# Half products of a 7-product matmul with moving operand and PSUM output taken from the last column to the first

## The chip, the cores and the metric

The kernel runs on one core of a Trainium2 chip. The metric is the device time of one execution in microseconds; the profile is that of one such execution, recorded by the hardware. A core has five engines with a queue of instructions each: TensorE (PE in the profile, its weight loads PEld), VectorE (DVE), ScalarE (ACT), GpSimd (POOL) and SyncE (SP), which issues DMAs. TensorE multiplies a stationary operand, held in its array, with a moving operand that it streams from SBUF column by column, and adds the result into PSUM.

## The reference, cut to what matters

One decoder layer on a sequence of 512 positions with a model width of 1024: a pooling mixer and a sparse attention in parallel, merged by gates, then a gated MLP with a short convolution. All inputs are fp32. The change lies in the first matmul of the MLP, `h @ w_up`:

```python
x = x + (gate_pool * y_pool + gate_nsa * y_nsa) @ w_out[l]
h = rms_norm(x, ffn_norm_g[l])
gate_pre, val = jnp.split(h @ w_up[l], 2, axis=-1)      # 1024 -> 2 x 2816
gate_c = causal_dwconv(gate_pre, conv_w[l], conv_b[l])  # 3 taps along the sequence
x = x + (jax.nn.silu(gate_c) * val) @ w_down[l]
```

## The kernel before, in words

**Layout.** Activations lie transposed: a feature block of 128 on the partitions, the 512 positions along the free dimension. A matmul has a 128x128 block of weights as its stationary operand and positions as its moving operand. Every fp32 number is split into a high and a low part, both of the type fp32r, and a product is the sum of three matmuls, high x high, high x low and low x high. ScalarE makes the high part by a rounding copy, and the low part comes from VectorE by a subtraction or from ScalarE and a DMA of GpSimd that adds.

**The MLP's first matmul.** The 2816 gate features and the 2816 value features are 22 blocks each; block `f` of both is worked on together. The first four blocks (`up_plain`) use 8 blocks of the model width times 3 matmuls of 512 columns, for gate and for value: 48 matmuls. Blocks 4 to 21 (`up_fast`) treat the same work as a 2x2 by 2x2 block product (gate and value x the two halves of the model width, by the two halves of the model width x the two halves of the positions) and do it with 7 products in place of 8, after a scheme of the Strassen kind. Each of the 7 is a call of `product` (L1133): 4 blocks of the inner width, and in each 3 matmuls of 256 columns, 12 matmuls in all. The sums of weight blocks that the scheme needs are made on VectorE, ScalarE and GpSimd for each `f`; those of the activations are made once, in `halves` (tiles `nh`, `nl` for the blocks as they are, `th`, `tl` and two reused tiles `ot`, `oraw` for the sums). `mov` returns for each product the moving half tile, 256 columns that lie next to each other in SBUF. The output of a product is the first 256 columns of a PSUM bank, `bank_[:, :H2]`; there are three banks per `f` (`bx`, `by`, `bq`), and two or three products add into each, with reads by ScalarE or VectorE in between.

**What sets the order.** The program is first recorded: each engine call becomes an operation of a plan (`Plan.note`, L382 is where all of them are issued in the end, so that all instructions of the profile carry that line). The plan simulates the engines with its own prices, several times, and emits the order that came out best. All matmuls of one block of one product are one unit. The price of a matmul depends on the number of columns of its moving operand, and the overlap of two accesses on the span of columns that they touch. Which semaphores an instruction waits for is derived when the operations are issued. A buffer of PSUM that is used again is waited for as a tile: the new user waits for all users of the old one.

**Beside the products.** Between the products of `up_fast` stand pieces of the MLP's second matmul (`dn_group`, 512 columns each, bank `sc`), and products 6 and 7 of a block `f` run inside the next block. After the last block come the rest of the second matmul and the stores.

Of the kernel before, what the change touches and what calls it, by code (L numbers as in the profile page):

```python
# [385 lines left out]
def hybrid_layer(ctx: ExitStack, tc: tile.TileContext, xT, pos, par, cst, poolw, w1, wa, wb, wf,  # L386
# [3 lines left out]
    PE, ACT, DVE, POOL, SP = pl.engines  # L390
# [16 lines left out]
    def keep(name, shape, dt=F32, bufs=1):  # L407
        return pl.tile(sb, shape, dt, name, "t_" + name, bufs)
# [250 lines left out]
    for t in range(NT):  # L659
        x, y = qp[t], kp[t]  # L660
# [156 lines left out]
    x = keep("kcx", (64, 1, DH))  # L817
# [247 lines left out]
    H2 = T // 2  # L1065
# [41 lines left out]
    def split_y(f, y):  # L1107
        yh[f], yl[f] = page("yh", dt=F32R), page("yl", dt=F32R)
        split(yh[f], yl[f], y)

    def up_plain(f):
# [18 lines left out]
        DVE.tensor_mul(y, y, t)  # L1130
        split_y(f, y)

    def product(bank_, a, b, k0):  # L1133
        ah, al = a
        bh, bl = b
        for k in range(4):
            c = slice(k * P, (k + 1) * P)
            with pl.unit():
                for j, (w, x) in enumerate(((ah, bh), (ah, bl), (al, bh))):
                    PE.matmul(bank_[:, :H2], w[:, c], x(k), start=k0 and k == 0 and j == 0,  # L1140
                              stop=k == 3 and j == 2, skip_group_check=True)

    def mov(i, half):
# [34 lines left out]
    def up_fast(f, n1, n2, n3):  # L1178
# [30 lines left out]
        p1, u2, u3 = half[0][:, :H2], half[0][:, H2:], half[1][:, :H2]  # L1209
        g, y = page("fg"), page("y")  # L1210
        product(bx, halves_(a1, 0), mov(0, 0), True)
        begun.append(pl.last())
        ACT.activation(p1, bx[:, :H2], AF.Copy)
        more = list(held)
        del held[:]
        if more:
            more[0]()
        fill(n1, f == PLAIN)
        product(by, h2, mov(2, 1), True)
        DVE.tensor_add(u2, by[:, :H2], p1)  # L1220
        if more:
            more[1]()
        fill(n3)
        product(bq, h1, mov(2, 0), True)
        product(bx, halves_(a1, 1), mov(1, 0), False)
        ACT.activation(g[:, :H2], bx[:, :H2], AF.Copy)
# [133 lines left out]
```

## Time and profile before

| what | value |
|---|---|
| median of 3 runs | 706.78 us |
| lowest and highest | 706.33 and 707.64 us |
| profiled execution | 706.15 us, its span 704.4 us |
| mean granted clock of TensorE | 0.999 |
| TensorE busy | 697.2 us of the span, 4142 matmuls |
| VectorE, ScalarE, GpSimd busy | 492.7, 422.3 and 103.7 us |
| moved by DMA | 113.99 MB |

How to read it: a group of instructions is given with the engine, the operation, output and inputs by the names of their tiles (buffer numbers left out), the shapes, the count, then busy time in us and the mean duration of one in ns, and what the engine waited for before them. The duration of a matmul runs from its start until its last column is in PSUM; the next matmul starts earlier, so the distance between starts is shorter than the duration. A tile that is written in PSUM has the name of its bank's group (`mm`, `tr`, `av`, `sc`). The chain is followed back from the last instruction, at each step to what released it.

### The profile page before, as it was taken

Reading aid. Unit: us, or ns where it says so; the run is one execution under the profiler, and the core shown is the slowest. Engines: PE = TensorE matmul, PEld = TensorE weight load, DVE = VectorE, ACT = ScalarE, POOL = GpSimd, SP = SyncE. Lnnn points to the kernel's source line nnn. Section 1 sums busy time; section 2 is a strip of 40 time slices with the busy share of each in tenths; the row PEclk is TensorE's granted clock in tenths of the full one; section 3 lists DMA queues with packets and bytes.
Section 4 is the critical chain, followed back from the end, with each engine's and each line's share of the span. In section 5 each row is a group of like instructions: output and inputs, shape, how many; then the busy total and the mean of one; then the engine's idle time right before and its main releaser. Section 6 shows DMA issues by size and latency. Waiting matters only on the chain.

```text
span 704.4 us, 11308 instructions
## 1 busy us (share of the span) xinstructions
PE 697.2 (99%) x4142; PEld 615.6 (87%) x4142; DVE 492.7 (70%) x1060; ACT 422.3 (60%) x756; POOL 103.7 (15%) x127
## 2 busy tenths in 40 slices
PE   9999999999999999999999999999999999999997
PEld 8898888888888888888888899999989999999886
DVE  6768488887866653675569967886778777776632
ACT  8557367677776664333467857685757566673310
POOL 0001301010110000000021323231312112220000
PEclk9999999999999999999999999999999999999999
DMA  8477255454565567844369698989868666774131
GB/s 297 167 180 224 61 120 135 105 132 109 150 153 143 146 139 229 280 158 156 122 150 235 151 211 170 219 185 222 186 173 205 157 162 166 170 161 112 45 127 60
DMA packets 45272, 113.99 MB, mean 162 GB/s; under 512 B 5281, under 2 KB 5409, under 8 KB 45217
## 3 DMA queue, kind: packets, MB, share of 16 engines
q1 hardware_dynamic: 29232, 76.57, 33.6%
q0 software_dynamic: 15840, 36.71, 29.1%
q8 instruction: 32, 0.52, 0.3%
q14 instruction: 24, 0.19, 0.1%
q10 hardware_dynamic: 144, 0.01, 0.0%
HBM read 70.27 MB, written 6.29 MB: 109 GB/s over the span
## 4 chain that ended last, share of the span: by engine, by line
PE 88%; DMA 3%; issue 3%; DVE 3%; ACT 1%; POOL 1%; POOLq 0%; ACTq 0%; DVEq 0%
PE mm L382 39%; PE tr L382 28%; PE sc L382 12%; PE av L382 10%; DMA sl<-r 2%; DMA r<-wup 1%; DVE wlo L382 1%; DMA sl<-wraw 0%; ACT whi L382 0%; DVE y L382 0%; POOL tl L382 0%; POOL sl L382 0%; ACT ft L382 0%; ACT sh L382 0%; DVE kc L382 0%
## 5 line engine op out<-in xcount | busy, mean ns | idle before, releaser
L382 ACT ACTIVATE whi<-wraw 128x1024 fp32r<-128x1024 f32 (+1 forms) x96 | 97.9, 1019 | 74.4 <-issue 29.0
L382 DVE TENSOR_TENSOR wlo<-wraw,whi 128x1024 fp32r<-128x1024 f32 (+1 forms) x66 | 76.4, 1157 | 16.6 <-ACT whi L382 14.3
L382 POOL DMA_DIRECT2D wlo<-wraw x30 | 26.3, 875 | 332.0 <-ACT wlo L382 278.7
L382 PE MATMUL mm<-xh,whi 128*128 128x512 f32 x176 | 73.0, 415 | 0.3
L382 PE MATMUL mm<-xh,wlo 128*128 128x512 f32 x176 | 69.0, 392 | 0.0
L382 PE MATMUL mm<-xl,whi 128*128 128x512 f32 x176 | 69.0, 392 | 0.0
L382 PE MATMUL mm<-tl,sh 128*128 128x256 f32 x190 | 53.8, 283 | 0.0
L382 PE MATMUL mm<-th,sh 128*128 128x256 f32 x174 | 49.5, 285 | 1.3 <-DVE u L382 1.2
L382 PE MATMUL mm<-th,sl 128*128 128x256 f32 x174 | 49.3, 284 | 0.2 <-DMA sl<-r 0.2
L382 POOL DMA_DIRECT2D sl<-r x36 | 31.4, 872 | 72.8 <-ACT sl L382 46.7
L382 ACT ACTIVATE pp<-pp,asm 128x128 f32<-128x128 f32 (+3 forms) x64 | 35.4, 556 | 11.1 <-DVE asm L382 11.0
L382 DVE SCALAR_TENSOR_TENSOR ft<-fg,pr,ft 128x511 f32<-128x511 f32 (+1 forms) x44 | 33.0, 749 | 11.8 <-ACT ft L382 11.1
L382 PE MATMUL sc<-yh,whi 128*128 128x512 f32 x104 | 40.8, 392 | 0.0
L382 PE MATMUL sc<-yl,whi 128*128 128x512 f32 x104 | 40.8, 392 | 0.0
L382 ACT ACTIVATE wlo<-wraw 128x1024 fp32r<-128x1024 f32 x30 | 31.8, 1060 | 14.9 <-PE mm L382 6.0
L382 PE MATMUL sc<-yh,wlo 128*128 128x512 f32 x104 | 40.5, 389 | 0.0
L382 PEld LDWEIGHTS mm<-xh,wlo 128*128 128x128 f32 x176 | 33.0, 188 | 7.3
L382 PEld LDWEIGHTS mm<-xh,whi 128*128 128x128 f32 x176 | 33.2, 189 | 5.8 <-DVE th L382 1.0
L382 PEld LDWEIGHTS mm<-xl,whi 128*128 128x128 f32 x176 | 33.3, 189 | 4.0
L382 PEld LDWEIGHTS mm<-tl,sh 128*128 128x128 f32 x190 | 36.4, 192 | 0.4
L382 PEld LDWEIGHTS mm<-th,sh 128*128 128x128 f32 x174 | 33.2, 191 | 3.1 <-DVE u L382 1.9
L382 ACT ACTIVATE ft<-fg,pr 128x512 f32<-128x512 f32 x22 | 17.8, 811 | 27.6 <-DVE fg L382 22.0
(394 smaller groups left out, 2116.9 us busy)
## 6 DMA issues: line engine op xcount, KB each, us to landing
wlo<-wraw POOLq DMA_DIRECT2D x30, 512.0 KB, 4.5
wraw<-wup SPq DMA_DIRECT2D x26, 512.0 KB, 4.3
wraw<-wf SPq DMA_DIRECT2D x22, 512.0 KB, 3.4
r<-wup SPq DMA_DIRECT2D x36, 256.0 KB, 4.7
sl<-r POOLq DMA_DIRECT2D x36, 256.0 KB, 5.3
wraw<-wdn SPq DMA_DIRECT2D x16, 512.0 KB, 4.5
sl<-s POOLq DMA_DIRECT2D x18, 256.0 KB, 6.2
sl<-wraw POOLq DMA_DIRECT2D x18, 256.0 KB, 4.3
```

Source lines behind the costliest of these rows:

```text
L382: getattr(self.real[o.eng], method)(*a, **kw)
```

## The change

A new helper `back` takes a two-dimensional access pattern (partitions, then columns with step 1) and returns one over the same elements that starts at the last column and has the step -1. In `product`, the moving operand and the PSUM output of every matmul go through it. Column 255 of the moving half tile is read first and lands in column 255 of the output, column 0 comes last; each result stands where it stood. The stationary operand, every other matmul of the kernel and all readers of the banks keep their patterns.

```diff
+    def back(x):
+        n = x.ap[1][1]
+        return bass.AP(tensor=x.tensor, offset=x.offset + n - 1, ap=[list(x.ap[0]), [-1, n]])
+
     def product(bank_, a, b, k0):
         ah, al = a
         bh, bl = b
@@
             with pl.unit():
                 for j, (w, x) in enumerate(((ah, bh), (ah, bl), (al, bh))):
-                    PE.matmul(bank_[:, :H2], w[:, c], x(k), start=k0 and k == 0 and j == 0,
+                    PE.matmul(back(bank_[:, :H2]), w[:, c], back(x(k)), start=k0 and k == 0 and j == 0,
                               stop=k == 3 and j == 2, skip_group_check=True)
```

In the program that comes out, the instructions of every engine and their order are the same as before. TensorE's matmuls have 44 more waits on TensorE's own semaphore, and 6 more instructions that only wait for it.

## The prediction

> **What bounds the kernel now.** I read the page first, its busy shares, its slices and the chain that ended last.
>
> ```profile
> span 704.4 us, 11308 instructions
> ...
> PE 697.2 (99%) x4142; PEld 615.6 (87%) x4142; DVE 492.7 (70%) x1060; ACT 422.3 (60%) x756; POOL 103.7 (15%) x127
> ...
> PEclk9999999999999999999999999999999999999999
> ...
> DMA packets 45272, 113.99 MB, mean 162 GB/s; under 512 B 5281, under 2 KB 5409, under 8 KB 45217
> ...
> PE 88%; DMA 3%; issue 3%; DVE 3%; ACT 1%; POOL 1%; POOLq 0%; ACTq 0%; DVEq 0%
> ```
>
> TensorE is busy for 99% of the span, at full granted clock in every slice, and it is 88% of the chain. So the kernel is bound by the rate at which TensorE takes matmuls, and whatever each matmul costs more or less is paid almost in full. That must hold in the stretch that the change touches, so I asked for the groups by shape between 380 and 670 us, and for the busy time between 384 and 667 us.
>
> ```profile
> L382 PE MATMUL mm<-tl,sh 128*128 128x256 f32 x190 | 53.8, 283 | 0.0
> ...
> L382 PE MATMUL mm<-th,sh 128*128 128x256 f32 x174 | 49.5, 285 | 1.3 <-DVE u L382 1.2
> L382 PE MATMUL mm<-th,sl 128*128 128x256 f32 x174 | 49.3, 284 | 0.2 <-DMA sl<-r 0.2
> ...
> L382 PE MATMUL tr<-oraw,sl 128*128 128x256 f32 x2 | 0.6, 283 | 0.0
> ```
> ```profile
> 384.00:667.00 283.00, 281.50 (x1948) 1.00 0.74 170
> 667.00:704.40 37.40, 33.47 (x148) 0.98 0.26 88
> ```
>
> The view has 24 groups of shape 128x256 there; their counts add up to 1512 matmuls. That is what the code gives: features 4 to 21 are 18 features, each with 7 products of 4 blocks and 3 matmuls, 18 x 84 = 1512. The stretch is 283.00 us long and TensorE is busy for 281.50 of it, so 1.50 us of idle time is all that a slower matmul could hide in; the last 37.40 us have no half product in them.
>
> The mean of one (283 ns) is a latency: the next matmul starts long before. What counts is the distance between starts, and the chain in order of time gives it, for merged runs of matmuls. The first row below is a run of half products, the second one of 512 columns (the output projection).
>
> ```profile
> 411.73 5.76 PE tr L382 x48
> 307.16 5.44 PE mm L382 x24
> ```
>
> 5.76 / 48 = 120.0 ns for 256 columns; 5.44 / 24 = 226.7 ns for 512 columns. The difference is 106.7 ns for 256 columns, 0.417 ns per column, and what is left of the 120.0 ns is a fixed part of 13.3 ns. The half products cost 1512 x 120.0 ns = 181.4 us now.
>
> **The change, part by part.** (1) The helper that builds the two patterns runs while the program is recorded and issues nothing. (2) The listing of the two programs has the same instructions in the same order on every engine. No DMA, no ScalarE, VectorE or GpSimd instruction differs, nothing is moved past a queue, and the planner's prices see the same number of columns. Cost 0. (3) The listing with waits shows one side effect: TensorE has 50 more waits on its own semaphore, 44 on the first matmul of a product and 6 in instructions of their own. Each waits for a matmul that stands at least 73 matmuls earlier, 73 x 120 ns = 8.8 us before, and that matmul's latency is 0.283 us. They are met long before they are asked. Such waits stand in the old program too (61 of them, on matmuls 13 to 124 places earlier), and the view of who waited for whom does not show a single one on TensorE:
>
> ```profile
> PE mm L382 <- DVE u L382: 1.2, 2, 0.6
> PE mm L382 <- POOL ones L382: 1.0, 1, 1.0
> PE tr L382 <- DVE qs L382: 0.2, 1, 0.2
> PE tr L382 <- ACT qt L382: 0.2, 1, 0.2
> PE mm L382 <- DMA sl<-r: 0.2, 1, 0.2
> ```
>
> So 0 again. If that cover were gone, and each of the 50 let the array run empty, it would cost the latency less the distance of starts, 283 - 120 = 163 ns, and 50 x 163 ns = 8.2 us; behind each waits only TensorE's own queue, and then every engine that evacuates the banks.
>
> (4) What remains is the work itself: 1512 moving reads and 1512 PSUM writes go from column 255 to column 0. No row of before has a matmul with a descending pattern, so this price has to be bounded from both sides.
>
> From above: the one matmul in this kernel whose moving operand is not read with step 1 is the compression's first layer, which takes every eighth column, 62 of them. The timeline has it in runs of 16:
>
> ```profile
> 74.83 1.99 PE L382 MATMUL tr<-kcb,w 128*128 128x62 f32 x16
> 76.57 0.48 PE L382 MATMUL mm<-xh,whi 128*128 128x512 f32 x1
> ```
>
> 76.57 - 74.83 = 1.74 us for 16, 108.8 ns each. A stepped column costs at most 108.8 / 62 = 1.75 ns, four times the forward 0.417; how much less is hidden, since a load of 128 weight columns alone may take these 108.8 ns. With 1.75 ns per column a half matmul would take 256 x 1.75 + 13.3 = 461 ns, 341 ns more, and 1512 of them 516 us more. From below: if the fixed 13.3 ns went away, these same 108.8 ns would remain as the shortest distance seen, so at most 11.2 ns are gained, 1512 x 11.2 ns = 16.9 us. The change therefore lies between -17 us and +516 us, and nothing in between is excluded by a row.
>
> Which value do I take? [...]
>
> ```profile
> L382 ACT ACTIVATE whi<-wraw 128x1024 fp32r<-128x1024 f32 x80 | 84.4, 1054 | 48.2 <-issue 29.0 <-PE mm L382 5.6 <-PE tr L382 5.1
> L382 ACT ACTIVATE sh<-wraw 128x512 fp32r<-128x512 f32 x36 | 22.4, 621 | 7.0 <-DVE wraw L382 6.4 <-ACT sh L382 0.6
> ```
>
> (1054 - 621) / 512 = 0.846 ns per element. TensorE's 0.417 ns per column is half of that (0.49): it seems to read and write two neighbouring columns in one such beat, which is my reading of the two slopes and not something that a row shows. If the two of a pair are joined only in ascending order, a descending stream goes one column per beat, 0.833 ns, whether the read or the write loses its pairs (both at once is no dearer, as they run in step). A half matmul then takes 256 x 0.833 + 13.3 = 226.7 ns, as long as a forward matmul of 512 columns. I take this value: it is the nearest one below the upper end that a slope of this trace supports, and a plain step of -1 has the whole of the stream, not its edge, to act on.
>
> The sum: 1512 x 106.7 ns = 161.3 us, less the 1.5 us of idle time that the stretch has now and that other engines then fill, +159.8 us. The profiled execution took 706.15 us, so 706.15 + 159.8 = 866 us. The median of the runs, 706.78 us, is 0.09% above that execution; I leave this out. Nothing takes the bound over: VectorE, ScalarE and the queues do the same work in a longer span (1512 matmuls longer, DMA at 113.99 MB / 864 us = 132 GB/s in place of 162), so they are only earlier for their due times, and the last 37.40 us stay as they are.
>
> [...]
>
> **The rivals.** No change, the rival on the other side: columns are fetched and written in pairs that are found by their address, whichever of the two comes first. Columns 255 and 254 lie side by side just as 0 and 1 do, the half tile starts and ends on an even boundary, and the pair is complete at every beat. For it speaks that the stepped read above is not visibly slow; against it that this row is hidden under its weight load. One property decides: whether a pair is found by its address or by an ascending step. Then every half matmul keeps its 120.0 ns and the time is 706.15 us, within 704.7 to 707.6. That the pattern would be turned back to ascending order on the way to the chip comes to the same number; the program still has the step -1 on operand and output of all 1512, so I give it no chance of its own. [...]
>
> A small cost: the stream keeps its rate and only the fixed part grows, by a late first column or by the 50 waits. At 5.4 ns per matmul, or with all 50 waits at 163 ns, this is 8.2 us, 714 us; doubling the fixed part (13.3 ns x 1512 = 20.1 us) gives 726 us. For it speaks that 13.3 ns are there already without an explanation; against it that the waits view has no wait of TensorE on itself.
>
> A cost far beyond half rate: every column pays a full access, up to the 1.75 ns of the upper end, 706.15 + 516 - 1.5 = 1221 us. The stepped row allows it and does not ask for it.
>
> A gain: the fixed part shrinks, 706 down to 689 us. Nothing in the profile points there.
>
> **How the numbers follow.** I give half rate 0.46, no change 0.22, a small cost 0.14, far beyond half rate 0.11, a gain 0.07. The time is that of half rate, 866 us; its own range is 850 to 886 us (the upper end if the fixed part doubles too: 2 x 120.0 ns, +181.4 us less 1.5; the lower one if one beat in ten still takes a pair). The range for 8 in 10 reaches from the no-change case through the small cost to half rate, 704.7 to 886 us, and leaves out the gain and the far cost, 0.18 together. 0.2% is about what runs of this kernel can tell from no change, as the three shown lie within 706.33 and 707.64. Slower by more than that: 0.46 + 0.14 + 0.11 = 0.71; within: 0.22; faster: 0.07.
>
> **What would show it.** The rows to compare are these, two of the chain in order of time and one group of full matmuls.
>
> ```profile
> 640.03 2.88 PE tr L382 x24
> 648.67 2.75 PE sc L382 x12
> ```
> ```profile
> L382 PE MATMUL sc<-yh,whi 128*128 128x512 f32 x104 | 40.8, 392 | 0.0
> ```
>
> Runs of 24 half matmuls take 2.88 us now; at half rate they take 5.4 to 5.5 us, with no change 2.88, and 12 matmuls of 512 columns keep 2.75 us in every case. The groups of shape 128x256 would go from 283 to about 390 ns, the latency that a 512-column matmul has now, with TensorE still at 99% and the clock at 9 in all slices. Gaps at the first matmul of products, with TensorE named as its own releaser, would point to the waits. The prediction is wrong if the half matmuls keep 120 ns apart, or go beyond 240 ns.

## The result and the profile after

The changed kernel takes 704.80 us (median of 18 runs, 702.29 to 706.52), the kernel before 706.73 us (18 runs, 705.02 to 707.64). The ratio is 0.9974, with a 95% interval of 0.9963 to 0.9984: 0.26% faster, where 23% slower was forecast. The profiled execution took 702.29 us and is the fastest of its kernel, so a difference of the two profiles shows more than the medians do.

The page of the changed kernel, its head, its chain and one group of half products:

```profile
span 700.5 us, 11314 instructions
PE 692.8 (99%) x4142; PEld 611.7 (87%) x4142; DVE 492.5 (70%) x1060; ACT 421.9 (60%) x756; POOL 103.4 (15%) x127
...
PE 89%; DMA 6%; DVE 2%; issue 1%; ACT 1%; SPq 0%; POOLq 0%; DVEq 0%; ACTq 0%
...
L382 PE MATMUL mm<-tl,sh 128*128 128x256 f32 x190 | 53.5, 282 | 0.0
```

TensorE is the bound as before, and the mean duration of one half matmul of this group has gone from 283 to 282 ns, not to 390. The chain in order of time, late in the products, with the start, the length and the count of each merged run:

```profile
636.43 2.84 PE tr L382 x24
639.27 1.42 PE av L382 x12
...
644.95 2.72 PE sc L382 x12
```

2.84 us for 24 is 118.3 ns from start to start, where 2.88 us was 120.0 ns. The twelve forward matmuls of 512 columns that follow, which the change does not touch, have gone from 2.75 to 2.72 us as well. The starts themselves show a rhythm. These are distances in ns within one product of 12, and within the group of 512 columns behind it, read off the starts in the two traces:

```
before  half:  120 120 120 120 120 120 120 120 120 120 120 120
        512:   234 235 229 232 231 227 226 227 227 226 227 227
after   half:  118 117 122 116 118 117 122 116 119 116 123 116
        512:   227 227 226 227 227 226 227 227 226 227 227 226
```

So a descending stream does not fall to half rate. It is 1.7 ns shorter per half matmul, and the 13.3 ns that the prediction called a fixed part are the first thing to ask about.

Not all of the 3.9 us between the two spans belongs to the change. The first half product of all begins at 395.90 us before and at 394.81 us after: 1.09 us had gone ahead of the first changed instruction. From there to the end of the last product it is 266.30 against 263.54 us, 2.76 us less, and the tail is 42.18 and 42.16 us.

### The profile page after: what moved, and what is told of

It reads as the page before. It is cut to its first block, busy times and chain, and to the rows that moved or that the text cites. A ratio compares the mean times of both kernels' runs of the same rounds, so it can differ in the third digit from the quotient of the medians.

```text
span 700.5 us, 11314 instructions
## 1 busy us (share of the span) xinstructions
PE 692.8 (99%) x4142; PEld 611.7 (87%) x4142; DVE 492.5 (70%) x1060; ACT 421.9 (60%) x756; POOL 103.4 (15%) x127
## 4 chain that ended last, share of the span: by engine, by line
PE 89%; DMA 6%; DVE 2%; issue 1%; ACT 1%; SPq 0%; POOLq 0%; DVEq 0%; ACTq 0%
PE mm L382 38%; PE tr L382 29%; PE sc L382 12%; PE av L382 11%; DMA r<-wup 4%; DMA sl<-r 2%; DVE wlo L382 0%; DMA wraw<-wa 0%; SPq L382 0%; DVE kc L382 0%; ACT ft L382 0%; DVE th L382 0%; DVE r L382 0%; DVE u L382 0%; DVE ft L382 0%
```

## The experiments

Three explanations of the gain were put against each other: the descending stream itself (A), the 50 added waits (B), a pace that belongs to the execution and that either program may meet (C). The first four kernels separate them and also take read and write apart; their diffs are against the changed kernel. With the read alone or the write alone reversed, the columns of each half come out in reverse order.

**The changed kernel once more** (no edit).

> The changed kernel once more, nothing else edited. Three theories for the 0.26%: (A) a descending stream leaves a shorter fixed part behind each half matmul; (B) the 50 added waits of TensorE on itself shift where its matmuls start; (C) the pace is a property of the execution, in which either program may fall. In the first profile the half matmuls started 118.3 ns apart on average (12 of a product in 1.42 us), before it was 120.0 ns (1.44 us). A and B: 1.42 us per product again, and about 0.997 of the kernel before. C: the profile may as well show 1.44 us, and the ratio comes nearer to 1.

Measured: 704.74 us against 706.35 us, ratio 0.9979 (0.9965 to 0.9994); its profiled execution took 706.31 us.

**The read alone.**

```diff
-PE.matmul(back(bank_[:, :H2]), w[:, c], back(x(k)), ...
+PE.matmul(bank_[:, :H2], w[:, c], back(x(k)), ...
```

> Only the moving half tile is read from the last column to the first; PSUM is written forward, so that the columns of each half come out in reverse order and the output of the layer is another one. This program has none of the 50 added waits. A, if it lies in the read: 1.42 us per product and 0.997 of the kernel before; if it lies in the write: 1.44 us and 1.000. B: 1.44 us and 1.000. C: either pace.

Measured: 704.69 us, ratio 0.9974 (0.9963 to 0.9985).

**The write alone.**

```diff
-PE.matmul(back(bank_[:, :H2]), w[:, c], back(x(k)), ...
+PE.matmul(back(bank_[:, :H2]), w[:, c], x(k), ...
```

> Only PSUM is written from the last column to the first; the moving half tile is read forward, so that the columns of each half come out in reverse order and the output of the layer is another one. This program has the 50 added waits. A, if it lies in the write: 1.42 us per product and 0.997; if in the read: 1.44 us and 1.000. B: 1.42 us and 0.997. C: either pace.

Measured: 706.12 us, ratio 0.9998 (0.9985 to 1.0012).

**The waits alone.**

```diff
+    def two(x):
+        n = x.ap[1][1] // 2
+        return bass.AP(tensor=x.tensor, offset=x.offset, ap=[list(x.ap[0]), [n, 2], [1, n]])
-PE.matmul(back(bank_[:, :H2]), w[:, c], back(x(k)), ...
+PE.matmul(two(bank_[:, :H2]), w[:, c], x(k), ...
```

> All columns forward as before, but the PSUM output of the half products is written down as two runs of 128 columns that lie next to each other: the same addresses in the same order, and the same 50 waits as in the changed kernel. The result is that of the reference. A: 1.44 us per product and 1.000 of the kernel before. B: 1.42 us per product and 0.997. C: either pace.

Measured: 706.45 us, ratio 0.9999 (0.9985 to 1.0013).

The chain in order of time gives the pace of each; a run of 24 half matmuls and the next one of 512 columns. First the read alone, then the write alone, then the waits alone:

```profile
638.27 2.84 PE tr L382 x24
646.79 2.72 PE sc L382 x12
```
```profile
635.96 2.75 PE sc L382 x12
638.71 1.43 PE mm L382 x12
640.14 2.88 PE tr L382 x24
```
```profile
639.46 2.88 PE tr L382 x24
635.28 2.75 PE sc L382 x12
```

The read alone has the pace and the gain, without one of the added waits. The write alone and the waits alone have neither. B falls. C falls for the products: with the waits taken out, the stretch of the products has one length for each direction of the read, in every profile. The table is worked out from the starts of the 1512 half and 360 full matmuls between the first and the last product; what a distance has above 124 ns (half) or 237 ns (full) is counted as waiting.

| kernel | first product starts | stretch | of it waiting | rest |
|---|---|---|---|---|
| before | 395.90 | 266.30 | 2.71 | 263.58 |
| waits alone | 395.88 | 265.74 | 2.18 | 263.56 |
| write alone | 394.60 | 267.71 | 4.13 | 263.58 |
| changed | 394.81 | 263.54 | 2.89 | 260.64 |
| changed, again | 395.99 | 266.38 | 5.70 | 260.69 |
| read alone | 395.38 | 264.80 | 4.14 | 260.66 |

(All in us.) The descending read is worth 2.9 us, and nothing else in the table moves the last column. The medians gained 1.93 us (changed), 1.61 us (changed, again) and 1.66 us (read alone). What lies between can be in the column of waits, which changes from execution to execution by up to 3.5 us; with one profile of each this is not shown for the medians. The waits view of the second profile of the changed kernel has 3.8 us on VectorE and 0.4 us on a DMA where before had 1.2 and 0.2.

```profile
PE mm L382 <- DVE u L382: 3.8, 3, 1.8
PE mm L382 <- DMA sl<-r: 0.4, 1, 0.4
```

C is alive outside the products. The 96 matmuls of 280 columns near 41 us, forward in all kernels, took 12.88 us in two of these six profiles and 12.35 us in four, without regard to the edit.

**The price of a pattern by itself.** A new kernel that holds its operands in SBUF and runs sections of equal matmuls back to back.

```diff
+    section("fwd")
+    section("rd", rstep=-1)                 # moving read descending
+    section("rdwr", rstep=-1, wstep=-1)
+    section("wr", wstep=-1)                 # PSUM write descending
+    section("wgap", pair=2)                 # pairs of columns, gaps of two
+    section("wpair", pair=True)             # neighbours swapped
+    section("rtwo", rstep=2)                # also -2, 4, 8
+    section("shone", shift=1)               # moving tile 1 column later; also 8, 64, 256
```

> A kernel that computes nothing of the layer: it loads one block of weights and four of x, splits them, and runs sections of 96 half matmuls (48 where they have 512 columns) back to back with nothing else on the chip's engines, each section with other patterns, in one order and then in the reverse order. Sections: forward; read descending; read and write descending; write descending; write in pairs of two columns with a gap of two; write in swapped pairs; read with step 2, -2, 4, 8; read forward with the half tile moved by 1, 8, 64 or 256 columns; read descending moved by 256; 512 columns forward and descending. In the layer a forward half matmul stands 120.0 ns from the next and one with a descending read 118.3. If the difference belongs to the two read streams of TensorE alone, forward is 120 and descending about 118.3 here too, and the sections that are moved by some columns say whether the place of the tile matters. If it belongs to what the other engines and DMAs do to the memory, both are equal here. Pairing theory of the prediction: a pair is found by its address, so swapped pairs cost nothing, while reads with step 2, 4 and 8, one column of each pair, take 0.83 ns per column, 227 ns. Lines wider than a pair would show in a price that goes on rising from step 2 to 4 or 8.

The chain in order of time has one row for each section (96 half matmuls: 11.52 us is 120.0 ns each, 11.36 us is 118.3):

```profile
19.48 11.52 PE fwd L382 x96
31.00 11.36 PE rd L382 x96
42.36 11.36 PE rdwr L382 x96
53.72 11.51 PE wr L382 x96
65.23 11.52 PE wgap L382 x96
76.75 11.52 PE wpair L382 x96
88.27 21.76 PE rtwo L382 x96
110.03 22.40 PE rtwod L382 x96
132.43 22.40 PE rfour L382 x96
154.83 20.91 PE reight L382 x96
175.74 11.82 PE shone L382 x96
187.56 11.21 PE sheight L382 x96
...
233.16 10.89 PE full L382 x48
244.05 11.20 PE fullrd L382 x48
```

With nothing else at work but one copy by ScalarE behind each section, the two paces of the layer come back to the tenth of a ns, 120.0 and 118.3 ns, so they belong to TensorE's own reads. A read that leaves out every second column takes 226.7 ns (21.76 / 96), which is the half rate of the prediction: it fits the author's reading that columns go in pairs and that a pair can be broken, which no row shows by itself. A descending read does not come near it (118.3 ns). Steps 4 and 8 cost about what step 2 costs (233.3 and 217.8 ns), so the price does not go on rising with the step. The write is free in every order tried here (11.51 and 11.52 us, 119.9 and 120.0 ns). And the direction is not what counts: a forward read one column later takes 123.1 ns (11.82 / 96), eight columns later 116.8 ns, and for 512 columns descending is the slower one (233.3 against 226.9 ns).

**The place of the two reads.** The same kernel with the tiles moved.

```diff
+    section("base")
+    section("sfour", shift=4)               # moving tile 4 columns later; also 2, 6, 8 ... 32
+    section("rdone", rstep=-1, shift=1)
+    section("weight", wshift=8)             # stationary block 8 columns later
+    section("wseight", wshift=8, shift=8)   # both
+    section("deight", dshift=8)             # PSUM output 8 columns later
```

> Again no computation of the layer, only sections of 96 half matmuls (48 of 512 columns), forward except where named: the moving half tile at a place 0, 2, 4, 6, 8, 12, 16, 24 or 32 columns after a 512-column boundary; descending from the same place, and from 1 and 8 columns later; the stationary block moved by 8 columns; both moved by 8; the PSUM output moved by 8; 512 columns moved by 8 and 16, and descending, moved by 1 and 8. If the pace is set by the column at which a read starts, relative to some block of memory, then it changes with the place in steps or waves, comes back to 120.0 ns at the period of that block (32 or 64 columns), a descending read from a moved place has another pace than 118.3, and moving the stationary block does nothing. If it is set by how the two reads of TensorE meet, moving both by 8 gives 120.0 again and moving the stationary block alone changes the pace. If it is the direction alone, the descending sections are all 118.3 and the moved forward ones between 116.7 and 123.3 as in the runs before have another cause. The output's place does nothing in any of them.

```profile
19.53 11.52 PE base L382 x96
31.05 11.52 PE stwo L382 x96
42.57 11.20 PE sfour L382 x96
...
87.85 11.31 PE ssixteen L382 x96
...
144.73 11.52 PE rdone L382 x96
156.25 11.37 PE weight L382 x96
167.62 11.50 PE wseight L382 x96
179.12 11.50 PE deight L382 x96
...
371.49 10.89 PE bssixteen L382 x96
...
427.67 11.21 PE bstwo L382 x96
```

Moving the stationary block by 8 columns, with the moving read left alone, changes the pace (11.37 us); moving both by 8 restores it (11.50 us); moving the output does nothing (11.50 us). A descending read one column later is back at 120.0 ns. A forward read 32 columns on stands at 118.6 ns in both orders, 64 and 256 columns on (kernel before this one) at 120.0; 6 and 24 columns on (11.51 and 11.52 us) stand there too, so a period was not shown. The pace goes with where the moving read and the stationary block stand to each other (120.0, 118.4 and 119.8 ns for none, one and both moved), as in the second of the three theories that the expectation names. The rows whose names begin with `b` are the same sections run in the reverse order: a place 16 columns on was at 117.8 ns the first time and at 113.4 ns (10.89 / 96) the second, and 2 columns on at 120.0 and 116.8 ns. One pattern can have two paces. The state in which the stream enters it is one explanation; the second pass also writes another PSUM bank, and only the layer below tells the two apart. The third theory of the expectation, direction alone, falls here. One more row of the reverse order, for the last section: 512 columns read descending from one column later.

```profile
235.31 11.31 PE bfrdone L382 x48
```

**Other orders, alone and in the layer.** If place is what counts, an order can be chosen for its pace, since the write follows any order at no cost.

```diff
+    section("dfour", b=4, kind='d')   # blocks of 4 from last to first, forward inside
+    section("sfour", b=4, kind='s')   # neighbouring blocks of 4 swapped
+    section("reight", b=8, kind='r')  # blocks of 8 forward, descending inside
```

> No computation of the layer, sections of back-to-back half matmuls (48 of 512 columns at the end), where read and write take the columns in another order: d, blocks of 4, 8, 16, 32 or 64 columns from the last to the first, forward inside; s, each two neighbouring blocks swapped; r, blocks forward, descending inside. If the pace is set by how the moving read and the weight load meet in memory, then what counts is the place in its period at which a read starts and how it runs on from there: d and s in blocks of 4 or 8 columns start off the place of the forward read and change the pace (116 to 119 ns), blocks of 64 start where the forward read starts and stay at 120.0. If a descending step as such were what helps, only the r sections get below 120. If every line of memory is fetched once and any order inside it is free, none of them is near the 227 ns of a stepped read. For 512 columns nothing below 226.7 has been seen; an order that goes below would be worth more in the layer than the change itself.

```profile
88.19 10.91 PE sfour L382 x96
99.09 12.80 PE seight L382 x96
...
146.31 11.52 PE rfour L382 x96
157.83 10.91 PE reight L382 x96
168.74 12.80 PE rsixteen L382 x96
...
271.26 12.80 PE fseight L382 x48
...
444.24 11.52 PE breight L382 x96
...
514.50 11.52 PE bsfour L382 x96
```

Swapped blocks of 4 and descending blocks of 8 reach 113.6 ns (10.91 / 96) the first time and 120.0 the second; swapped blocks of 8 take 133.3 ns, and 266.7 ns for 512 columns (12.80 / 48). Read and write took the new order together, so these prices are not divided between them. One place of the expectation was missed: blocks of 8 taken from the last to the first were to leave 120.0 ns and stay there (11.52 us). No order of 512 columns came below the forward 226.7 ns. The two best orders went into the layer:

```diff
-ap=[list(x.ap[0]), [-1, n]]                       # offset n - 1
+ap=[list(x.ap[0]), [8, n // 8], [-4, 2], [1, 4]]  # offset 4: swapped blocks of 4
+ap=[list(x.ap[0]), [8, n // 8], [-1, 8]]          # offset 7: descending blocks of 8
```

> The whole layer, with the result of the reference: in the half products, moving read and PSUM write take the columns 4 to 7, 0 to 3, 12 to 15, 8 to 11 and so on, each two neighbouring blocks of four swapped. Alone this order was at 113.3 ns or at 120.0, by what ran before it. If the pace alone sets the layer's time and the faster mode is met, a product takes 1.36 us, and 1512 x 6.7 ns = 10.1 us go: 696 us, 0.986 of the kernel before. In the slower mode: 1.44 us and 1.000. If TensorE, made faster, only waits longer for its weights in the first fast features, less than half of the 10.1 us shows.

> The same with blocks of eight columns taken forward and descending inside each: 7 to 0, 15 to 8, 23 to 16 and so on. Alone it too was at 113.3 or at 120.0. In the faster mode 1.36 us per product and 0.986 of the kernel before, in the slower 1.44 us and 1.000. If a step of -1 in itself were what made the changed kernel faster, this one, whose steps are nearly all -1, would be like it: 1.42 us and 0.997.

Measured: swapped blocks of 4 take 700.78 us, ratio 0.9917 (0.9901 to 0.9933); descending blocks of 8 take 701.56 us, 0.9919 (0.9903 to 0.9934); the kernel before 707.12 us beside them. Both are faster than the kernel before and than the changed one. Chain rows of the two, swapped blocks first:

```profile
639.84 2.72 PE tr L382 x24
642.56 1.36 PE av L382 x12
```
```profile
633.92 2.72 PE tr L382 x24
636.64 1.36 PE av L382 x12
```

2.72 / 24 = 113.3 ns: the layer is mostly in the faster of the two paces. By the starts, 1363 of the 1512 half matmuls with swapped blocks and 1353 with descending blocks stand 113 or 114 ns from the next. The slower pace is there too: with the descending blocks, 55 in a row stand 120 ns apart from 422.77 us on, behind a wait for a DMA, and the stream is back at 113.3 ns behind the next group of 512 columns. The pattern did not change there and the run of 55 goes over banks of the groups `tr`, `mm` and `av`, all of which stand at 113.3 ns elsewhere. How the stream enters fits this, and the bank does not. The blocks of 8, whose steps are nearly all -1, are at 113.3 and not at the 118.3 ns of the changed kernel, so a step of -1 as such is not what helps. By the accounting of the table above, the rest of the stretch is 254.20 and 254.26 us, 9.4 us below the forward one. The medians gained 6.3 us (swapped) and 5.6 us (descending), more than half of the 10.1 us that the expectation gave, and short of its 696 us. The remainder can go into waits of TensorE for a bank that VectorE still reads; before, these came to 1.2 us. The waits view of the swapped blocks, then of the descending ones:

```profile
PE mm L382 <- DVE u L382: 6.8, 5, 3.0
PE tr L382 <- DMA sl<-r: 0.3, 1, 0.3
```
```profile
PE mm L382 <- DVE u L382: 3.2, 3, 1.3
```

The first is the slowest execution of its kernel (705.18 us) and the second the fastest (699.25 us), so neither shows where the median lost its part. In the first, about 1.5 us more are no wait at all: eight matmuls of 512 columns near 520 us start 427 ns apart, and the granted clock of this stretch, the first figure behind the count, is 0.58.

```profile
518.50:522.60 4.10, 4.10 (x15) 0.58 0.41 140
```

## Why the prediction was wrong, step by step

The forecast was 866 us. The median of 704.80 us lies 0.1 us inside the lower end of the range for 8 in 10, an end that was set by the rival "no change"; it says nothing for the half rate.

**What bounds the kernel** held: TensorE at 99%, and 1512 half matmuls that pay nearly in full. The pace before, 120.0 ns, was read rightly and came back in a kernel of its own.

**Parts 1 to 3 held.** The order is the same, and the waits cost nothing: the kernel with the waits alone is at 0.9999, and no profile has TensorE waiting for itself.

**Part 4 failed, at the choice between the bounds.** The prediction took half rate from two slopes: two columns per beat going forward, hence one per beat going back. Both slopes were read rightly, and half rate exists, 226.7 ns to the tenth of a ns at step 2. The pairs were the author's estimate from those two slopes. No run shows the 0.833 ns per column of the forecast's sum as a pace of a descending stream, nor that ScalarE's 0.846 ns per element says anything of TensorE; the runs showed 118.3 ns for a descending half matmul. The step from "pairs" to "pairs in ascending order only" had no row behind it, and it is the part that was wrong: a descending read does not fall to half rate (118.3 ns, so 1.7 ns less per half matmul where the prediction added 106.7 ns), and swapped or gapped pairs on the write side cost nothing (120.0 ns). The upper bound, at most 1.75 ns per column for step 8, was true and loose by a factor of two: (217.8 - 13.3) / 256 = 0.80 ns.

**The rival "no change" had what matters for the size**: no half rate going back (118.3 ns). Its mechanism, a pair found by its address, was not shown; it fits the rows as far as half rate goes: that came with steps of 2, 4 and 8 columns alone (226.7, 233.3 and 217.8 ns). Its 706.15 us is 0.2% above the measured median. It had no place for the 1.7 ns. For the write, only orders that keep two neighbouring columns one behind the other were tried; single columns with gaps between them were not, so what PSUM takes for them is open.

**The rival "a gain" had the sign.** It was given 0.07 because "nothing in the profile points there". The fixed part of 13.3 ns was there to ask about, and it is no fixed part. The distance of half matmuls changes with where the moving read and the weight load stand to each other and with the order of the columns; it ran from 113.3 to 133.3 ns in sections that read 256 neighbouring columns. Nor is 0.417 ns per column a rate that stays. Split by the prediction's own way, from 256 and 512 columns, the descending read gives (233.3 - 118.3) / 256 = 0.449 ns per column and 3.3 ns left over, and swapped blocks of 8 give (266.7 - 133.3) / 256 = 0.521 ns and nothing. So two lengths of one order do not tell a rate from a fixed part here. The lower bound of the prediction, 108.8 ns from the 62-column rows, was not crossed by any section.

The section with the stationary block moved by 8 columns went from 120.0 to 118.4 ns and with both moved back to 119.8 (11.50 / 96): here the two reads are not independent. What exactly meets was not settled. The runs show that the relative place counts, that one pattern can run at two paces (113.6 and 120.0 ns for swapped blocks of 4), and nothing of the parts inside.

## What to carry to other kernels

A number that is left over after the rate is accounted for is a question, not a constant: find out what it depends on before carrying it through a sum, and price a second order of the columns before taking the slope between two lengths for a rate. Where a matmul stream with a new stationary block each time is the bound, try the order or the place of the moving columns, with PSUM written in the same order: here it gave 0.8% for a changed access pattern, and it can as well lose 13 ns a matmul (133.3 against 120.0 ns for swapped blocks of 8, in the short kernel). Between two bounds far apart, price the pattern alone in a short kernel rather than take the more telling of two stories.

## What was not expected of the hardware

- Most paces that do not vary within a section are whole multiples of 6.67 ns: 113.3 and 120.0 ns for 256 columns, 226.7, 233.3 and 266.7 ns for 512 columns or step 2 (17, 18, 34, 35 and 40 times). One is not: 512 columns descending from one column later take a steady 235.6 ns (11.31 / 48). Others, like 118.3 ns, are averages over a rhythm.
- The pace of forward matmuls differed with the half products ahead of them: twelve of 512 columns took 2.75 us behind a forward product and 2.72 us behind a descending one.
- The same untouched matmuls of 280 columns ran at one of two paces in the six profiles of the table, 12.88 or 12.35 us for 96.
